# Queries, keys and values of three heads moved into the gate units, attention moved beside the r projection

## The chip, the cores and the metric

The kernel runs on one core of a Trainium2 chip. The metric is device microseconds of one execution. Each core has a matrix engine (PE, with its weight loads PEld), a vector engine (DVE), an activation engine (ACT), a general engine (POOL), and SyncE (SP), which here issues all DMAs, in program order.

## The reference

One encoder layer, 1024 tokens by 1024 channels, float32. Cut to what matters here:

```python
h = rmsnorm(x, norm_mix)
q, k, v, r, lr_f, lr_b, u, g_a, g_b = split(h @ w_in)     # 512 512 1024 1024 16 16 512 1024 1024
log_a_f = log_sigmoid(lr_f @ w_decay_up_fwd + b_decay_fwd) / 16      # and _b
# 4 heads of 128 keys and 256 values
o = gla_chunked(qh, kh, vh, af, include_diag=True) + flip(gla_chunked(flip(qh), flip(kh), flip(vh), flip(ab), False))
o = o * rsqrt(mean(o * o) + EPS) * gla_norm * silu(r)
y_a = o @ w_branch_gla
y_b = pooled(u) @ w_pool_group * pool_scale
x = x + (sigmoid(g_a) * y_a + sigmoid(g_b) * y_b) @ w_out
x = x + swiglu(rmsnorm(x, norm_ffn), w_ffn_in, w_ffn_out)
return rmsnorm(x, norm_final)
```

`gla_chunked` needs, per head and direction, the running sum of `log_a` within each chunk of 64, its exponentials on q and k, a masked score product, and a state carried from chunk to chunk.

## The kernel before

A float32 product is made of three matmuls on values split into a high and a low part (hi x hi, lo x hi, hi x lo): `products` and `mm3` (L268 to L275). A weight tile is loaded raw, cast to its high part on ACT (L197) and its difference taken on POOL or DVE (L198).

The work before the branch projection comes in this order on PE:

- Norms of the eight token tiles, and v of head 0 token tile by token tile (`values`, L384: 24 matmuls of 256 columns for a tile).
- The low-rank product `lrT` (L449), 32 matmuls.
- For each head h: q and k (`project_qk`, feature-major, 24 matmuls of 512 columns for each half of the tokens), then v of heads 1 to 3 by `values`. `attention(h)` is begun beside them as a side generator.
- r (`feature_major`, eight column tiles, two halves each), with the gated output (`gated`, L966: transposes of the head's output, one DVE operation) and the loads of the heads' outputs, which went to HBM (`o_out`).
- Ten gate units (u0, u1, four of g_A, four of g_B), each two column tiles wide. A unit computes a 2 x 2 block product (two column tiles, two halves of h's 1024 channels against two halves of the tokens) with seven half-size products instead of eight, each of 12 matmuls of 512 columns. Products 1 to 7 need sums and differences of weight blocks (fs, L882, on DVE) and of blocks of h (`right`). `Ahead` runs the weights' preparation some steps ahead (five). Pooling and the remaining sums run beside the units as generators.
- `project(0, BRANCH, ...)`: the branch projection by the same scheme, with blocks of `ob`, the gated output, as the left operand.

Four mechanisms set where other work stands. `pump(dt)` (L158) is called after every few matmuls and advances three lists: `pending` weight splits; `aside`, jobs on DVE, ACT and POOL with a pace (a new job every so many units of `dt`, only while no split is pending); and `side`, generators whose `yield` gives the wait in the same units until their next step. `finish_side` and `finish_beside` emit all that is left at once. `later` puts a DMA on a list and `flush` issues the list on SP. An engine runs its instructions in the order they were emitted; a DMA that must wait holds what stands behind it on SP.

`beside` (L572) runs a list of jobs: `branch_jobs` and `output_jobs` each make four generators, whose sums (wsum, L600, on POOL) of weight blocks go to HBM (`s_out`, `t_wo`) and are loaded by the branch and output projections; `feature_jobs` makes the sums of blocks of h (`hs`, `trh`, `trl`, L585 and L600, on DVE) that the units use as their right-hand side.

`attention(h)`: for each half and direction `decay` (z matmul, scan on DVE), `exponentials`, `apply_decay` (qe, ke), transposed keys (kt), a backward sweep over the chunks that saves the states (sb), then the forward sweep that makes the output (op, o), with its square sum, and `rms_scale` (ors, on POOL, L303).

Of the kernel before, what the change touches and what calls it, by code (L numbers as in the profile page):

```python
# [17 lines left out]
P = 128  # L18
D = 1024
SEQ = 1024  # L20
KT = D // P
# [30 lines left out]
def kernel(  # L52
# [354 lines left out]
    v = value_slots()  # L407
    norm_x(0)
# [34 lines left out]
    prepare()  # L443
    lrT = slot(F32R, (2, HALF), "lrT")
    for half in range(2):
        ps = bank(ps_mm)
        for k in range(KT):
            for i in range(2):
                nc.tensor.matmul(  # L449
                    ps[:, :], lw[k // 4][:, k % 4, :, :].rearrange("p a r -> p (a r)"), hT(k, half)[i],  # L450
                    start=k == 0 and i == 0, stop=k == KT - 1 and i == 1,
                )
            pump(2 / 3)
        nc.scalar.copy(lrT[:, half, :], ps[:, :])
        nc.vector.tensor_tensor(lrT[64:96, half, :], ps[64:96, :], as_f32(lrT[64:96, half, :]), op=ALU.subtract)


# [9 lines left out]

# [150 lines left out]
    v_heads, o_heads, unscaled = {}, {}, []  # L618
    HOLD, SCORES = 4.4, 6

    def project_qk():
        q = slot(s="q")
        k = slot(s="k")
        for dst, scale in ((q, DK**-0.5), (k, 1.0)):
            w = take()
            for half in range(2):
                ps = feature_major(w, hT, half)
                nc.scalar.activation(dst[:, half, :], ps[:, :], AF.Copy, scale=scale)
        return q, k

    def attention(h, q, k):


        qe = [slot(s="qe") for _ in range(2)]
        ke = [slot(s="ke") for _ in range(2)]
        fac = {}
        runs = ((1, 1), (0, 1), (0, 0), (1, 0))
        zs, las = {}, {}
        for half, d in runs:
            z = bank(ps_g, "z")  # L640
            nc.tensor.matmul(z[:, :], up[:, h, d, :], lrT[:, half, :], start=True, stop=True)
            bias = b_dec[d][:, h : h + 1]
            la = t2(s="la")
            nc.vector.tensor_scalar(la[:, :], z[:, :], bias, 0.0, op0=ALU.add, op1=ALU.min)
            nc.scalar.activation(z[:, :], z[:, :], AF.Abs, bias=bias)
            zs[half, d] = z
            las[half, d] = la
            yield 1.3
        for run in runs:
            nc.scalar.activation(zs[run][:, :], zs[run][:, :], AF.Exp, scale=-1.0)  # L650
        if unscaled:
            unscaled.pop()()
        yield 3.5
        flush()
        for run in runs:
            nc.scalar.activation(zs[run][:, :], zs[run][:, :], AF.Ln, bias=1.0)
        yield 6.5

        totals = {}

        def decay(half, d):
            la, z = las[half, d], zs[half, d]
            nc.vector.tensor_tensor(la[:, :], la[:, :], z[:, :], op=ALU.subtract)
            cs = z
            tot = vec(8, "tot")
            cs3 = cs.rearrange("p (n c) -> p n c", c=SUB)
            la3 = la.rearrange("p (n c) -> p n c", c=SUB)
            cy = carry.rearrange("p n c -> p (n c)")
            if d == 0:
                nc.vector.tensor_tensor_scan(cs[:, :], cy, la[:, :], 0.0, op0=ALU.mult, op1=ALU.add)  # L670
                nc.vector.tensor_copy(tot[:, :], cs3[:, :, SUB - 1])
            else:

                nc.vector.memset(cs[:, 0:1], 0.0)
                nc.vector.tensor_tensor_scan(  # L675
                    cs[:, 1:], la[:, : HALF - 1], cy[:, 1:], 0.0, op0=ALU.add, op1=ALU.mult
                )
                nc.vector.tensor_tensor(tot[:, :], cs3[:, :, SUB - 1], la3[:, :, SUB - 1], op=ALU.add)
            first = cs.rearrange("p (n a c) -> p n a c", a=2, c=SUB)[:, :, 0, :]
            tot2 = tot.rearrange("p (n a) -> p n a", a=2)  # L680
            nc.vector.tensor_tensor(first, first, tot2[:, :, 0:1].broadcast_to([P, 4, SUB]), op=ALU.subtract)
            totals[half, d] = tot

        def exponentials(half, d):
            cs, tot, e_q = zs[half, d], totals[half, d], qe[half]
            f = vec(12, "fac")
            sign = INV_NORMALIZER if d == 0 else -INV_NORMALIZER
            nc.scalar.activation(e_q[:, d, :], cs[:, :], AF.Exp, scale=sign)
            nc.scalar.activation(cs[:, :], cs[:, :], AF.Exp, scale=-sign)
            nc.scalar.activation(f[:, :8], tot[:, :], AF.Exp, scale=INV_NORMALIZER)  # L690
            fac[half, d] = f

        def apply_decay(half, d):
            f, e_q, e_k = fac[half, d], qe[half], ke[half]
            f2 = f[:, :8].rearrange("p (n a) -> p n a", a=2)
            nc.vector.tensor_tensor(e_k[:, d, :], zs[half, d][:, :], k[:, half, :], op=ALU.mult)
            nc.gpsimd.tensor_tensor(e_q[:, d, :], e_q[:, d, :], q[:, half, :], op=ALU.mult)
            nc.gpsimd.tensor_tensor(f[:, 8:], f2[:, :, 0], f2[:, :, 1], op=ALU.mult)

        def factor(n, d, which):  # L700
            f = fac[n // 4, d]
# [8 lines left out]

        def transposed_keys(half, d):
            kp = bank(ps_g, "kp")
            for i in range(4):
                nc.tensor.transpose(kp[:, i * P : (i + 1) * P], chunk_of(ke, 4 * half + i, d), ident[:, :])
            kt = slot(F32R, s="kt")
            split_to(kt[:, 0, :], kt[:, 1, :], kp[:, :])
            return kt
# [32 lines left out]
        decay(1, 1)  # L750
        yield HOLD
        exponentials(1, 1)
        decay(0, 1)
        yield 2
        apply_decay(1, 1)
        yield HOLD - 2
        exponentials(0, 1)
        decay(0, 0)
        yield 2
        apply_decay(0, 1)  # L760
        yield HOLD - 2
        exponentials(0, 0)
        kts = {(1, 1): transposed_keys(1, 1)}
        yield 1.5
        apply_decay(0, 0)
        decay(1, 0)
        yield HOLD
        while h not in v_heads:
            yield 0.5
        v = v_heads[h]  # L770

        def value(n):
            return tuple(part[:, n % 4, :] for part in v[n // 4])

        sb = [slot(shape=(4, DV), s="sb") for _ in range(2)]
        old = None
        for n in range(NT - 1, 0, -1):
            state, old = advance(old, n, 1, kts[n // 4, 1])
            m = n - 1
            nc.scalar.activation(  # L780
                sb[m // 4][:, m % 4, :], state, AF.Copy, scale=factor(m, 1, "before")
            )
            if n == 7:
                exponentials(1, 0)
            elif n == 5:
                apply_decay(1, 0)
            yield 1.2
            if n == 7:
                kts[0, 1] = transposed_keys(0, 1)
                yield 0.5  # L790
            if n == 2:
                kts[0, 0] = transposed_keys(0, 0)
                yield 0.5
# [5 lines left out]
        for n in range(NT):  # L799
# [18 lines left out]
            if n == 0:  # L818
                yield 0.38
                kts[1, 0] = transposed_keys(1, 0)  # L820
# [5 lines left out]
            yield 1.02  # L826
        rs = rms_scale(ms[:, :], NT, "ors")
        if h == HEADS - 1:
            o_heads[h] = o

        def normalize():
# [3 lines left out]
            if h < HEADS - 1:  # L835
                for half in range(2):
                    later(o_out[h][:, 4 * half : 4 * half + 4, :], o[half][:, :, :])

        unscaled.append(normalize)
        if h == HEADS - 1:  # L840
            unscaled.pop()()

    o_out = [dram.tile([P, NT, DV], F32, name=f"o_out{h}") for h in range(HEADS - 1)]

    def load_o(h):
        o_heads[h] = [slot(shape=(4, DV), s="ol") for _ in range(2)]
        for half in range(2):
            nc.sync.dma_start(o_heads[h][half][:, :, :], o_out[h][:, 4 * half : 4 * half + 4, :])

    for h in range(HEADS):  # L850
        qk = project_qk()
        begin(attention(h, *qk))
# [1017 lines left out]
```

## Time and profile before

| | |
|---|---|
| three runs | 1397.41, 1399.39, 1399.9 us |
| median | 1399.39 us |
| span of the profiled execution | 1400.4 us |
| matrix engine's matmuls | 6677 |
| DMA | 243.62 MB, mean 174 GB/s |

Its stages on PE: to 45 us norms and v of head 0; to 52 low rank; to 74 q, k of head 0; to about 335 heads, with attention; to 390 the rest of r; to 598 gate units; then branch, output projection and FFN. Durations of one matmul in groups are its latency; how fast they follow each other is seen in chains.

### The profile page before, as it was taken

What the parts mean: (1) busy time and instruction counts of PE and PEld (TensorE: products, weight loads), DVE (VectorE), ACT (ScalarE), POOL (GpSimd) and SP (SyncE); (2) the same over time, 40 slices, a digit from 0 to 9 for tenths busy, and PEclk for the clock granted to TensorE, in tenths of its full rate; (3) what the DMA queues carried; (4) which work ended last, traced back from release to release, by engine and by line L of the source; (5) the groups of instructions that cost most, each with busy time, mean ns of one, the idle gap of its engine ahead of it and who ended that gap; (6) DMA issues with size and microseconds to landing.
All of it is one profiled execution on the core that took longest, in us unless ns stands there. A gap on an engine that the chain in (4) does not pass through costs nothing.

```text
span 1400.4 us, 18571 instructions
## 1 busy us (share of the span) xinstructions
PE 1371.4 (98%) x6677; PEld 1157.4 (83%) x6677; DVE 854.4 (61%) x1073; ACT 624.6 (45%) x1119; POOL 750.4 (54%) x558
## 2 busy tenths in 40 slices
PE   7999999999999999999999999999999999999997
PEld 6889898988888878788887888888888888888876
DVE  6256857677745975587874865556565556343363
ACT  6364655554334444455346633333333334453253
POOL 3251616132288456468665176666666667454354
PEclk9999999999999999999999999999999999999999
DMA  6212413222368667996524455554444447975461
GB/s 193 76 45 61 136 59 107 89 79 71 125 207 286 199 220 235 346 407 233 194 76 173 173 180 174 173 173 156 145 142 148 140 153 255 388 255 218 165 234 67
DMA packets 167612, 243.62 MB, mean 174 GB/s; under 512 B 10936, under 2 KB 98016, under 8 KB 167520
## 3 DMA queue, kind: packets, MB, share of 16 engines
q1 hardware_dynamic: 167520, 242.45, 51.2%
q8 instruction: 52, 0.85, 0.2%
q14 instruction: 40, 0.33, 0.1%
HBM read 164.55 MB, written 77.86 MB: 173 GB/s over the span
## 4 chain that ended last, share of the span: by engine, by line
PE 81%; DVE 7%; ACT 4%; issue 3%; POOL 2%; DMA 2%; SPq 0%; POOLq 0%; DVEq 0%; ACTq 0%
PE ps L271 73%; PE op L813 2%; POOL wl L198 1%; PE kv L271 1%; PE sc L741 1%; PE op L271 1%; DVE z L670 1%; PE yb L271 1%; PE tr L318 1%; PE ps L449 1%; PE tp L972 1%; DMA gor<-g_out 0%; DMA wor<-t_out 0%; DVE z L675 0%; DMA u_out<-uph 0%
## 5 line engine op out<-in xcount | busy, mean ns | idle before, releaser
L198 POOL TENSOR_TENSOR wl<-fs,wh 128x512 fp32r<-128x512 f32 x120 | 165.9, 1386 | 163.4 <-ACT wh L197 138.1
L271 PE MATMUL ps<-gl,wh 128*128 128x512 f32 x616 | 239.8, 389 | 0.9 <-DVE gl L1462 0.9
L271 PE MATMUL ps<-gh,wh 128*128 128x512 f32 x616 | 240.4, 390 | 0.0
L271 PE MATMUL ps<-gh,wl 128*128 128x512 f32 x616 | 239.7, 389 | 0.0
L198 POOL TENSOR_TENSOR wl<-fraw,wh 128x512 fp32r<-128x512 f32 x90 | 129.1, 1435 | 63.9 <-ACT wh L197 63.9
L271 PE MATMUL ps<-hh,wh 128*128 128x512 f32 x376 | 150.4, 400 | 0.0
L198 POOL TENSOR_TENSOR ol<-gor,oh 128x1024 fp32r<-128x1024 f32 (+1 forms) x42 | 100.3, 2394 | 93.1 <-ACT oh L197 86.0
L271 PE MATMUL ps<-hh,wl 128*128 128x512 f32 x376 | 146.9, 391 | 0.0
L271 PE MATMUL ps<-hl,wh 128*128 128x512 f32 x376 | 146.8, 390 | 0.0
L198 POOL TENSOR_TENSOR wl<-raw,wh 128x512 fp32r<-128x512 f32 x47 | 64.4, 1382 | 152.8 <-ACT wh L197 141.4
L271 PEld LDWEIGHTS ps<-gl,wh 128*128 128x128 f32 x616 | 115.7, 188 | 25.0 <-DVE gl L1462 1.3
L271 PEld LDWEIGHTS ps<-gh,wl 128*128 128x128 f32 x616 | 115.7, 188 | 24.2
L271 PEld LDWEIGHTS ps<-gh,wh 128*128 128x128 f32 x616 | 115.7, 188 | 23.6
L271 PE MATMUL ps<-oh,oh 128*128 128x512 f32 x308 | 119.9, 389 | 1.3 <-DVE x L1792 1.3
L271 PE MATMUL ps<-ol,oh 128*128 128x512 f32 x308 | 119.9, 389 | 0.2 <-DVE ol L198 0.2
L271 PE MATMUL ps<-oh,ol 128*128 128x512 f32 x308 | 119.8, 389 | 0.0
L198 POOL TENSOR_TENSOR wl<-wraw,wh 128x512 fp32r<-128x512 f32 x56 | 90.9, 1653 | 45.4 <-ACT wh L197 36.1
L198 DVE TENSOR_TENSOR ol<-wor,oh 128x1024 fp32r<-128x1024 f32 (+1 forms) x42 | 62.0, 1496 | 53.9 <-ACT oh L197 46.6
L197 ACT CAST wh<-fs 128x512 fp32r<-128x512 f32 x120 | 73.8, 615 | 28.4 <-DVE fs L882 28.3
L271 PEld LDWEIGHTS ps<-hh,wl 128*128 128x128 f32 x376 | 70.8, 188 | 15.3
L271 PEld LDWEIGHTS ps<-hl,wh 128*128 128x128 f32 x376 | 71.1, 189 | 13.5
L271 PEld LDWEIGHTS ps<-hh,wh 128*128 128x128 f32 x376 | 71.1, 189 | 13.2
(251 smaller groups left out, 3197.4 us busy)
## 6 DMA issues: line engine op xcount, KB each, us to landing
fraw<-in_w_ffn_in_dram SPq DMA_DIRECT2D x44, 512.0 KB, 6.1
gor<-g_out SPq DMA_DIRECT2D x35, 512.0 KB, 6.3
raw<-in_w_in_dram SPq DMA_DIRECT2D x48, 256.0 KB, 3.1
g_out<-s SPq DMA_DIRECT2D x44, 256.0 KB, 2.3
fraw<-in_w_in_dram SPq DMA_DIRECT2D x20, 512.0 KB, 6.5
wor<-t_out SPq DMA_DIRECT2D x20, 512.0 KB
g_out<-g SPq DMA_DIRECT2D x33, 256.0 KB, 2.6
x<-in_x_dram SPq DMA_DIRECT2D x16, 512.0 KB, 4.9
```

The lines of the kernel that those rows point to most:

```text
L197: nc.scalar.copy(hi, src)
L198: eng.tensor_tensor(lo, src, as_f32(hi), op=ALU.subtract)
L271: nc.tensor.matmul(ps, a[i], b[j], start=first and n == 0, stop=last and n == 2, skip_group_check=onto)
L318: nc.tensor.transpose(ps[:, c], xt[:, k * P : (k + 1) * P], ident[:, :])
L449: nc.tensor.matmul(ps[:, :], lw[k // 4][:, k % 4, :, :].rearrange("p a r -> p (a r)"), hT(k, half)[i], start=k == 0 and i == 0, stop=k == ...
L670: nc.vector.tensor_tensor_scan(cs[:, :], cy, la[:, :], 0.0, op0=ALU.mult, op1=ALU.add)
L741: nc.tensor.matmul(sc[d][:, i * CH : (i + 1) * CH], chunk_of(ke, n, d), chunk_of(qe, n, d), start=True, stop=True,)
L813: nc.tensor.matmul(op[:, :DV], a, b, start=False, stop=j == len(terms) - 1)
L972: nc.tensor.transpose(tp[:, i * P : (i + 1) * P], o_heads[j // 2][half][:, i, (j % 2) * P : (j % 2 + 1) * P], ident[:, :],)
```

## The change

q, k and v of heads 1 to 3 become units among the gate units: 16 units, in the order u0, u1, q1 to q3 (each q and k of a head), v1 to v3, four of g_A, four of g_B. A q or v unit stores its results like a gate unit does; a v unit is transposed back to token-major by `turn` (16 transposes, one split) and put to HBM (`v_out`), q and k go to `qk_out`. The decays of all heads are made by a side generator, `decays`, beside the units and put to HBM (`dec_out`, 32 DMAs). r comes after the units, and the attention of all four heads beside it: `load_head`, `load_values` and `apply_decay` of the next head are called in the forward sweep of the one before. Half 1 of h is put to HBM (`h_out`) at the start and loaded back for r. The feature sums run beside low rank and q, k of head 0; `branch_jobs` and `output_jobs` run beside r, at pace 3. The outputs of heads 2 and 3 stay on chip for the branch projection. `Ahead` runs three steps ahead instead of five, and a unit's raw weights are loaded after product index 3, behind the flush, instead of index 0.

```diff
-    order = []
-    for h in range(HEADS):
-        cols_of = [(Q0 + h * DK, DK), (K0 + h * DK, DK), (V0 + h * DV, DV)]
-        order += [(w_in, KT, *c) for c in (cols_of if h else cols_of[2:] + cols_of[:2])]
-    order += [(w_in, KT, R0 + j * P, P) for j in range(KT)]
-    order = iter(order)
+    order = iter(
+        [(w_in, KT, c0, width) for c0, width in ((V0, DV), (Q0, DK), (K0, DK))]
+        + [(w_in, KT, R0 + j * P, P) for j in range(KT)]
+    )
...
-    prepare()
-    lrT = slot(F32R, (2, HALF), "lrT")
...
+    for half in range(2):
+        for n, part in enumerate(v[half]):
+            later(v_out[0][n][:, 4 * half : 4 * half + 4, :], as_f32(part[:, :, :]))
+    for kp in range(2):
+        for n, part in enumerate(hT.pair(kp, 1)):
+            later(h_out[kp][n], as_f32(part[:, :, :]))
+    flush()
...
+    def decays():
+
+        for h in range(HEADS):
+            for half in (1, 0):
...
+                for d in (1, 0):
+                    for n, t in enumerate((cums[d], las[d])):
+                        nc.sync.dma_start(dec_out[h][half][n][:, d, :], t[:, :])
+                yield 10
...
+            if h + 1 < HEADS:
+                if n == 2:
+                    load_head(h + 1)
+                if n == 4:
+                    load_values(h + 1, 1)
+                if 4 <= n < NT:
+                    apply_decay(h + 1, *RUNS[n - 4])
+                if n == NT - 1:
+                    load_values(h + 1, 0)
+                    kt_of[h + 1] = transposed_keys(h + 1, 1, 1)
+            yield STEP
         rs = rms_scale(ms[:, :], NT, "ors")
...
-    for h in range(HEADS):
-        qk = project_qk()
-        begin(attention(h, *qk))
-        if h == 0:
-            prepare_beside(map(branch_jobs, range(4)), 6)
-        if h > 0:
-            v = value_slots()
-            w = take()
-            for t in range(NT):
-                values(w, v, t)
-        v_heads[h] = v
...
+    kinds = [("u", i) for i in range(2)] + [("q", h) for h in range(1, HEADS)] + [("v", h) for h in range(1, HEADS)]
+    kinds += [(kind, i) for kind in "ab" for i in range(KT // 2)]
...
+    SUMS = 2.1
+    prepare_beside([feature_jobs(0), feature_jobs(1)], SUMS)
+    prepare()
+    lrT = slot(F32R, (2, HALF), "lrT")
...
+    project_qk(first_unit)
     finish_beside()
+    for _ in range(AHEAD - 3):
+        gates_ahead.step()
+    flush()
...
+        def turn(self, half):
+
+            hi, lo = slot(F32R, (4, DV), "vh"), slot(F32R, (4, DV), "vl")
+            for pair in range(2):
+                ps = bank(ps_g, "vt")
+                for t in range(2):
+                    for i in range(2):
+                        nc.tensor.transpose(
+                            ps[:, (2 * t + i) * P : (2 * t + i + 1) * P],
+                            self.row(i)[:, half, (2 * pair + t) * P : (2 * pair + t + 1) * P], ident[:, :],
+                        )
+                src = ps.rearrange("p (t c) -> p t c", t=2)
+                split_to(hi[:, 2 * pair : 2 * pair + 2, :], lo[:, 2 * pair : 2 * pair + 2, :], src[:, :, :])
+            for n, part in enumerate((hi, lo)):
+                later(v_out[self.at][n][:, 4 * half : 4 * half + 4, :], as_f32(part[:, :, :]))
...
-    for _ in range(AHEAD - 2):
-        gates_ahead.step()
-    flush()
+    begin(decays(), 4)
...
-            for _ in range(2 * (at == 0 and not last)):
-                gunits[n + 1].load()
...
-            if at == 4:
+            if at == 3:
                 flush()
...
+            for _ in range(2 * (at == 3 and not last)):
+                gunits[n + 1].load()
...
             if last and at == 1:
-                load_block(0, 0)
-                line_load()
-                line_load()
-                load_block(1, 0)
...
+                fetch()
+                load_head(0)
+            elif last and at == 4:
+                load_values(0, 1)
+                load_values(0, 0)
+                prepare()
...
+    for kp in range(2):
+        hT.tiles[kp, 1] = tuple(slot(F32R, s="h" + s) for s in "hl")
+        for n, t in enumerate(hT.tiles[kp, 1]):
+            nc.sync.dma_start(as_f32(t[:, :, :]), h_out[kp][n])
...
+    for h in range(HEADS):
+        begin(attention(h))
+    prepare_beside(chain(map(branch_jobs, range(4)), map(output_jobs, range(4))), 3)
+    for j in range(KT):
+        w = take()
+        r = slot(s="r")
+        for half in range(2):
+            ps = feature_major(w, hT, half)
+            flush()
+            nc.scalar.activation(r[:, half, :], ps[:, :], AF.Silu)
+            silu_r.append((j, half, r[:, half, :]))
+            for _ in range(2):
+                put_by()
+            if j == KT - 1:
+                if half == 0:
+                    finish_beside()
+                    load_block(0, 0)
+                    line_load()
+                    line_load()
+                else:
+                    load_block(0, 1)
+    finish_beside()
     project(0, BRANCH, collect_branch, before_branch)
```

More of the change, by code (lines that the diff above doesn't have):

```diff
@@ L442 @@
             low_rank_weights()
-    prepare()
-    lrT = slot(F32R, (2, HALF), "lrT")
[L445 to L455, printed above, removed]
     deferred = []
@@ L626, in project_qk @@
+    heads, v_heads, o_heads = {}, {}, {}
+    SCORES = 6
+    def project_qk(amid):
+        qk = [slot(s=s) for s in "qk"]
+        for dst, scale in zip(qk, (DK**-0.5, 1.0)):
+            w = take(dst is qk[0])
             for half in range(2):
+                amid(dst is qk[1], half)
                 ps = feature_major(w, hT, half)
                 nc.scalar.activation(dst[:, half, :], ps[:, :], AF.Copy, scale=scale)
[L629 to L653, printed above, removed]
-        flush()
[L655 to L698, printed above, removed]
@@ new lines, in project_qk, with load_head @@
+        for n, t in enumerate(qk):
+            later(qk_out[0][n], t[:, :, :])
+    def load_head(h):
+        q, k = (slot(s=s) for s in "qk")
+        qe, ke = {}, {}
+        for t, src in ((k, qk_out[h][1]), (q, qk_out[h][0])):
+            nc.sync.dma_start(t[:, :, :], src)
+        for half in (1, 0):
+            for n, (e, s) in enumerate(((qe, "qe"), (ke, "ke"))):
+                e[half] = slot(s=s)
+                nc.sync.dma_start(e[half][:, :, :], dec_out[h][half][n])
+        heads[h] = q, k, qe, ke
@@ L700, in factor, with attention @@
+    kt_of = {}
+    def attention(h):
+        q, k, qe, ke = heads[h]
         def factor(n, d, which):
-            f = fac[n // 4, d]
+            f = facs[:, h, n // 4, d, :]
             i = n % 4
@@ L709, in chunk_of @@
             return e[n // 4][:, d, (n % 4) * CH : (n % 4 + 1) * CH]
[L711 to L717, printed above, removed]
         def advance(old, n, d, kt):
@@ L748, in scores @@
             return hi, lo
[L750 to L770, printed above, removed]
-        def value(n):
-            return tuple(part[:, n % 4, :] for part in v[n // 4])
+        def value(n):
+            return tuple(part[:, n % 4, :] for part in v_heads[h][n // 4])
+        if h == 0:
+            for run in RUNS:
+                apply_decay(0, *run)
+                yield 1.5
+            kt_of[0] = transposed_keys(0, 1, 1)
+            yield 2
+        kts = {(1, 1): kt_of.pop(h)}
         sb = [slot(shape=(4, DV), s="sb") for _ in range(2)]
@@ L834, in normalize, with transposed_keys @@
                 nc.vector.tensor_scalar(t, t, rs[:, n : n + 1], None, op0=ALU.mult)
[L835 to L848, printed above, removed]
-    for h in range(HEADS):
-        qk = project_qk()
-        begin(attention(h, *qk))
-        if h == 0:
-            prepare_beside(map(branch_jobs, range(4)), 6)
-        if h > 0:
-            v = value_slots()
-            w = take()
-            for t in range(NT):
-                values(w, v, t)
-        v_heads[h] = v
+            o_heads[h] = o
+        soon(2, normalize)
+    STEP = 1.2
+    def transposed_keys(h, half, d):
+        ke = heads[h][3]
+        kp = bank(ps_g, "kp")
+        for i in range(4):
+            nc.tensor.transpose(kp[:, i * P : (i + 1) * P], ke[half][:, d, i * CH : (i + 1) * CH], ident[:, :])
+        kt = slot(F32R, s="kt")
+        split_to(kt[:, 0, :], kt[:, 1, :], kp[:, :])
+        return kt
     class Unit:
@@ L962 @@
     gates_ahead = Ahead(gunits, chain(*(steps_of(n, n == len(gate_units) - 1) for n in range(len(gate_units)))))
-    raw_r, oT = [], {}
-    def gated(j, half, src):
-        sr = t2(s="sr")
-        nc.scalar.activation(sr[:, :], src, AF.Silu)
-        tp = bank(ps_g, "tp")
-        for i in range(4):
-            nc.tensor.transpose(
-                tp[:, i * P : (i + 1) * P],
-                o_heads[j // 2][half][:, i, (j % 2) * P : (j % 2 + 1) * P], ident[:, :],
-            )
-        if j // 2 not in oT:
-            oT[j // 2] = [slot(s="o") for _ in range(2)], []
-        tiles, there = oT[j // 2]
-        nc.vector.scalar_tensor_tensor(
-            tiles[half][:, j % 2, :], tp[:, :], g_gla[:, j : j + 1], sr[:, :], op0=ALU.mult, op1=ALU.mult
-        )
-        there.append((j, half))
-        if len(there) == 4:
-            c = j // 2 % 2
-            for half, t in enumerate(tiles):
-                later(ob_out[j // 4, half][:, 2 * c : 2 * c + 2, :], t[:, :, :])
@@ L988, in put_by @@
-    def put_by():
-        if raw_r:
-            gated(*raw_r.pop(0))
-    BY = 3
-    sums_begun = False
-    for j in range(KT):
-        if 2 <= j <= 4:
-            load_o(j - 2)
-        w = take()
-        if j == 6:
+    SUMS = 2.1
[3 more added lines that the diff above has]
+    for half in range(2):
+        ps = bank(ps_mm)
+        for k in range(KT):
+            for i in range(2):
+                nc.tensor.matmul(
+                    ps[:, :], lw[k // 4][:, k % 4, :, :].rearrange("p a r -> p (a r)"), hT(k, half)[i],
+                    start=k == 0 and i == 0, stop=k == KT - 1 and i == 1,
+                )
+            pump(2 / 3)
+        nc.scalar.copy(lrT[:, half, :], ps[:, :])
+        nc.vector.tensor_tensor(lrT[64:96, half, :], ps[64:96, :], as_f32(lrT[64:96, half, :]), op=ALU.subtract)
@@ L1000, with first_unit @@
+    def first_unit(k, half):
+        if k and half == 0:
             for _ in range(2):
                 gunits[0].load()
[L1002 removed]
+        elif k:
             gates_ahead.step()
[L1004 to L1022 removed]
+    project_qk(first_unit)
@@ L1250, in run @@
             if part:
-                nc.scalar.copy(self.row(part[0])[:, part[1], :], ps)
+                nc.scalar.activation(self.row(part[0])[:, part[1], :], ps, AF.Copy, scale=self.scale(part[0]))
                 return
@@ L1377, in load_gates @@
                 nc.sync.dma_start(tiles[c][:, :, :], src[:, 1 - j, k : k + 2, :])
-    u2, v2 = ([slot(s="sum") for _ in range(2)] for _ in range(2))
     def merge(i, j, m, ps, s):
```

197 lines of the change are left out of this document (135 added, 62 removed).

## The prediction

> **What bounds the kernel now.** I read the page's first part, then the chain of waits, then the windows by stage, then groups by shape.
>
> ```profile
> span 1400.4 us, 18571 instructions
> PE 1371.4 (98%) x6677; PEld 1157.4 (83%) x6677; DVE 854.4 (61%) x1073; ACT 624.6 (45%) x1119; POOL 750.4 (54%) x558
> ```
>
> PE is the bound. The span is 1.0 us above the median of the runs (1399.39); I work against the span and take 1.0 off at the end. "Busy" hides pauses, so what a matmul costs is read from the chain of waits, where unbroken stretches stand with their count (start, length, what):
>
> ```profile
> 45.08 7.28 PE ps L449 x32
> 52.36 22.44 PE ps L271 x99
> ...
> 165.80 1.08 PE ps L271 x9
> ...
> 334.23 0.88 PE tp L972 x8
> 335.11 5.46 PE ps L271 x24
> ...
> 390.44 78.92 PE ps L271 x348
> ...
> 597.79 73.19 PE ps L271 x323
> ```
>
> A 512-column matmul costs 78.92 / 348 = 0.2268 us, a 256-column one 1.08 / 9 = 0.12, a transpose 0.88 / 8 = 0.11. The longer durations in the groups are latency. The branch projection begins at 597.79; everything the change touches lies before it.
>
> ```profile
> core 0: us, PE busy (x) PEld busy (x) DVE busy (x) ACT busy (x) POOL busy (x), PEclk, DMA share, GB/s
> 74.00:335.00 261.00, 257.17 (x1626) 232.82 (x1625) 179.03 (x343) 147.48 (x327) 99.91 (x84) 0.99 0.27 85
> 390.40:597.80 207.40, 204.18 (x890) 167.73 (x889) 131.59 (x148) 92.62 (x167) 134.61 (x103) 0.99 0.78 255
> 231.00:235.00 4.00, 3.60 (x12) 3.17 (x13) 3.83 (x7) 1.02 (x2) 3.92 (x4) 0.57 0.18 70
> 568.70:573.00 4.30, 4.25 (x12) 3.34 (x13) 0.88 (x2) 0.29 (x1) 3.08 (x4) 0.60 1.05 401
> ```
>
> In 74 to 335 (q, k, v of the heads with attention beside) the groups by shape, first and last of 16, are
>
> ```profile
> L271 PE MATMUL ps<-hh,wh 128*128 128x512 f32 x152 | 62.2, 409 | 0.0
> ...
> L972 PE MATMUL tp<-ident,ol 128*128 128x128 f32 x8 | 1.0, 272 | 0.0
> ```
>
> By width they are about 470 of 512 columns, 950 of 256 and 200 of 128: 470 x 0.2268 + 950 x 0.12 + 200 x 0.11 = 243 us. So 18 us of the 261 are lost. In 390.4 to 597.8 the 890 matmuls are worth 202 us, about 5.5 lost. **So PE loses some 23.5 us before the branch; this is all that better cover could return.** The named waits are few:
>
> ```profile
> PE kv L271 <- DVE kt L198: 3.4, 3, 2.1
> ...
> PE yb L271 <- DMA ph<-p_out: 1.0, 1, 1.0
> ...
> PE yb L271 <- DMA pl<-p_out: 0.8, 1, 0.8
> ```
>
> **The work removed.** Per head, 192 matmuls of 256 columns (v) and 96 of 512 (q, k) become two units of 7 x 12 = 168 of 512. Over three heads -576 x 0.12 = -69.1 and +216 x 0.2268 = +49.0. The v units come out feature-major and are turned back: 48 transposes, +5.3. Sum **-14.8 us**, from counts. The group that shrinks (256 before, 64 after, in each of three products):
>
> ```profile
> L271 PE MATMUL ps<-wh,hh 128*128 128x256 f32 x256 | 79.9, 312 | 0.0
> ```
>
> **The start.** Before, SP's list shows weight loads from 24.94 to 56.5 us, eight of them, those of q long landed; and ACT's list has q's cast while the low-rank product was on PE:
>
> ```profile
> 24.94 31.57 SPq L205 DMA_DIRECT2D raw<-in_w_in_dram  x8
> ```
>
> ```profile
> 49.26 0.62 ACT L197 CAST wh<-raw 128x512 fp32r<-128x512 f32 x1
> ```
>
> After, SP meets four puts of v and four of h (512 KB each) ahead of q's weight loads. The last two v puts wait for v's last split, at about 46. Six puts, 3 MB, at the 401 GB/s of the full stretch above are 7.8 us; the loads are issued near 48.2, share the transfers, and land at about 55.5 to 56, with the cast 57. q would have begun at 52.36, so PE waits about 5 us (bounds 1 and 7). Behind that cast on ACT stands the low-rank copy.
>
> The right-hand sums for unit 0 are made beside this stretch now, on DVE, where before they ran beside r:
>
> ```profile
> L600 DVE TENSOR_TENSOR hs<-hs,hs 128x1024 f32<-128x1024 f32 x8 | 11.8, 1481 | 0.2
> ...
> L600 DVE TENSOR_TENSOR hs<-hh,hl 128x1024 f32<-128x1024 f32 x8 | 10.7, 1351 | 0.0
> ...
> L585 DVE TENSOR_TENSOR trl<-hs,trh 128x1024 fp32r<-128x1024 f32 x8 | 10.6, 1342 | 8.6 <-DMA ob_out<-o 5.6 <-ACT trh L594 3.1
> ```
>
> 24 operations, 33.1 us, begun near 58 behind the late cast: the last pair is ready at about 90. Without loss PE would start unit 0 at 74 and read that pair near 78, with 5 us of the first wait at 83: 7 more. Start together **+12** (4 to 14).
>
> **The units before r.** Six units of q, k, v: weights' differences are on POOL and DVE as in the gate units, which lost nothing in the 78.92 us row; but each turn waits for an ACT copy and a split, like kt. By that row a wait is 3.4 / 3 = 1.1: three v units **+3.4** (0 to 7). The a and b units lose 5.5 now; the steps ahead fall from 5 to 3, the next weights are asked for three products later and behind the flush, and the decays' 32 puts precede. A few waits of the size of ph and pl: **+3** (-2 to +8).
>
> **Start of r.** Half 1 of h is loaded back, on SP behind the last yb puts:
>
> ```profile
> yb_out<-ga SPq DMA_DIRECT2D x8, 512.0 KB, 7.5
> ```
>
> The last put has its data some 3 us after the last product (sigmoid, gating, both behind the sum); issue 1.5 and a landing of about 6, less than the 7.5 since fewer are under way, make 10.4; r's half 0, which has its input on chip, covers 5.9 (24 matmuls and the first of the scan). **+4.5** (0 to 8).
>
> **Attention beside r.** Its DVE need per head: now 179.03 / 4 = 44.8, less the decays, less v's split, plus the gated output:
>
> ```profile
> L670 DVE TENSOR_TENSOR_SCAN z<-carry,la 128x512 f32<-128x512 bf16 x8 | 14.4, 1802 | 0.3
> L675 DVE TENSOR_TENSOR_SCAN z<-la,carry 128x511 f32<-128x511 f32 x8 | 13.8, 1731 | 0.3
> ...
> L644 DVE TENSOR_SCALAR la<-z,cols 128x512 f32<-128x512 f32 x16 | 11.7, 746 | 22.4 <-PE z L641 22.4
> ...
> L979 DVE SCALAR_TENSOR_TENSOR o<-tp,cols,sr 128x512 f32<-128x512 f32 x16 | 11.3, 742 | 5.7 <-ACT sr L969 5.2 <-ACT wh L197 0.5
> L198 DVE TENSOR_TENSOR vl<-ps,vh 128x256 fp32r<-128x256 f32 x32 | 13.3, 421 | 21.5 <-ACT vh L197 21.2
> ```
>
> Scans 7.1, two la passes (the second taken as long as the quoted one) some 6.0, v 2.5, gated +3.0: 32.2 per head. PE's work beside it, counted: r 384 x 0.2268 = 87.1, 376 of 256 columns 45.1, 256 of 128 28.2, together 160.4, and 149 until the last head's last output: 37.3 per head. DVE is 86% needed, against 179.03 / 261 = 69% before. No decays in the chain, but more density: I take **-2** of the 18 lost (-10 to +10).
>
> **The end of r.** This decides. Eight sum generators (four of the branch, four of the out weights) run beside r at pace 3; four operations each on POOL, and each one's loads on SP queue behind the puts of the one before. When the last half of r begins, three are not done: 12 operations. POOL takes them in program order, behind head 3's ors power, which needs head 3's last output; after that output PE has 42 wide matmuls and 16 transposes left, 42 x 0.2268 + 16 x 0.11 = 11.3 us. SP holds the first ob and weight loads of the branch behind the last put.
>
> ```profile
> L600 POOL TENSOR_TENSOR wsum<-wsum,wsum 128x512 f32<-128x512 f32 x16 | 22.7, 1420 | 0.5
> L600 POOL TENSOR_TENSOR wsum<-wsum 128x512 f32<-128x512 f32 x16 | 21.5, 1344 | 0.4
> ...
> L303 POOL TENSOR_TENSOR ors<-ors,half_neg 128x8 f32<-128x8 f32 x4 | 6.6, 1652 | 74.5 <-DVE ors L302 74.5
> ```
>
> ```profile
> DMA to landing us min/median/max: 2.4/3.5/7.7
> ```
>
> The second row is the landing of wsum's transfers. Chain: square, ors and power 3.0; two operations 2.8; the next loads, issue and landing, 4.4; two operations 2.8; loads 4.4; four operations 5.5; two ob and two weight loads 6.4; cast and difference 1.2: 30.5, less 11.3, is **+19** (12 to 25; 6.4 is the least sure, since
>
> ```profile
> ob<-ob_out SPq DMA_DIRECT2D x8, 512.0 KB, 10.8
> ```
>
> shows longer). Before, these loads were issued some 18 us ahead of 597.8, in the last unit, so PE passed without a stop. ob of heads 2 and 3 stay on chip, which spares 2 MB behind this, where nothing waits.
>
> **The clock.** In 231 to 235 PE, after its 2.1 us wait for kt, was granted 0.57 on average: half clock for about 3.4 us, which costs 1.7. The same followed the ph and pl waits (0.60). New long stops are the start, r's start and r's end; in the first the second wait swallows the slow time: 2 x 1.7 = **+3.4** (0 to 7).
>
> [...]
>
> **Sum.** -14.8 + 12 + 3.4 + 3 + 4.5 - 2 + 19 + 3.4 = +28.5: span 1428.9, time 1427.9; the larger terms can share cover (late PE gives DMA time), so I take about 3 off: **1425**. The likeliest case's own range is 1410 to 1441.
>
> **Rivals.**
> - *SP's order does not bind.* All three stops (start, r's start, r's end) are loads behind puts. If the puts' data is ready some 10 us before the loads are needed, all go: 1428 - 12 - 4.5 - 19 - 3.4 = 1389, **faster**. For it: pieces of 512 KB often land in 3 to 5 us. Against: at r's end the puts' data hangs on POOL behind ors, and ors on PE. It decides from chain under 11.3 us. Chance 0.15.
> - *Only the end is covered* (POOL's operations pass ahead of ors in time, or fewer remain): 1425 - 21 = 1404, from 1394 to 1410. Chance 0.17, half of it above +0.2%.
> - *DVE becomes the bound beside r.* At 86% need, with its waits for POOL's products and reloaded decays, each head takes 4 us more: +16, about 1441 to 1455. For it the 3.4 us kt waits at 69%; against, r's matmuls are interleaved as filler. Chance 0.13.
> - *The saving itself is not there* (half products bring waits of their own for their split and adds): the 78.92 us row speaks against, 348 in a row without a pause. It would be 1440, inside the upper part. Chance 0.03.
>
> **Numbers.** Forecast 0.52. Slower: 0.52 + 0.13 + 0.03 + 0.09 = 0.77; within 0.2% (2.8 us, about what a measurement can tell): 0.05; faster: 0.15 + 0.03 = 0.18. The range 1392 to 1446 leaves out the first rival's lower half and the third's upper half, under 2 in 10.
>
> **What would show it.** Matmul groups of 64 x 256 columns and PE's count 312 lower; PE waiting for ACT's wh cast after low rank, for DVE's low part (trl) in unit 0, for hh and hl loads at r's start; above all a gap of 12 to 25 us at the head of the branch, with POOL in wsum and ob loads issued after its last put. Wrong if that gap is under 5 us, if PE before it passes the start without 4 us, or if attention beside r loses more than 30 us.

## The result and the profile after

| | median of the runs | ratio to before, 95% interval |
|---|---|---|
| before | 1399.64 us (1397.41 to 1401.53, 4 runs) | |
| after | 1517.45 us (1513.69 to 1518.15, 4 runs) | 1.0845 (1.0824 to 1.0866) |

The change makes the kernel 118 us slower. The forecast was slower, but by 25 us. First the page of the changed kernel:

```profile
span 1516.4 us, 18227 instructions
PE 1399.6 (92%) x6365; PEld 1145.4 (76%) x6365; DVE 881.5 (58%) x1103; ACT 649.5 (43%) x1138; POOL 768.9 (51%) x576
```

PE has 312 matmuls fewer, as counted (6677 to 6365), and is at 92% of a longer span instead of 98%. No other engine is full: DVE fell from 61% to 58%. So nothing became the bound by amount; PE waits. The windows by stage say where. Their edges are the first matmul of unit 0 that reads the new sums (94.7), the last of the units (470.5), the end of r (674.4), the first branch product (689.4) and the first FFN product (871.7):

```profile
core 0: us, PE busy (x) PEld busy (x) DVE busy (x) ACT busy (x) POOL busy (x), PEclk, DMA share, GB/s
45.10:94.70 49.60, 35.42 (x146) 28.00 (x144) 34.09 (x28) 14.59 (x21) 9.91 (x6) 0.89 0.45 143
94.70:470.50 375.80, 342.43 (x1437) 267.30 (x1438) 213.94 (x288) 200.01 (x350) 178.62 (x148) 0.97 0.55 183
470.50:674.40 203.90, 185.52 (x1023) 158.90 (x1022) 127.75 (x245) 74.16 (x176) 79.10 (x60) 0.95 0.58 194
674.40:689.40 15.00, 0.28 (x3) 0.04 (x1) 2.58 (x3) 1.72 (x4) 5.05 (x4) 0.60 0.85 297
689.40:871.70 182.30, 167.96 (x704) 134.89 (x705) 123.48 (x124) 82.26 (x135) 112.12 (x71) 0.94 0.50 179
871.70:1516.40 644.70, 633.29 (x2805) 522.99 (x2803) 351.49 (x351) 247.60 (x391) 372.83 (x242) 1.00 0.54 186
```

The same windows of the kernel before, from the first branch product on, show that the FFN is the same and the branch is not:

```profile
597.80:756.30 158.50, 156.55 (x704) 129.08 (x704) 121.41 (x125) 80.65 (x131) 109.59 (x69) 1.00 0.58 213
756.30:1400.40 644.10, 633.32 (x2805) 523.15 (x2803) 351.24 (x351) 249.03 (x392) 373.74 (x242) 1.00 0.54 186
```

With the matmul costs of the prediction each stretch can be split into work and loss. Units: 1389 wide matmuls and 48 transposes are 320 us, so 56 of 376 are lost (the gate units of before lost 5.5). r with attention: 160 of work, 43.5 lost (18 in the heads before). End of r: 15 us with nothing on PE. Branch and out projection: the same 704 matmuls take 23.8 us more. The start: 146 wide matmuls are 33 of 49.6 us, 16.5 lost, where before nothing was. Against before that is 50 + 25.5 + 15 + 23.8 + 16.5 - 14.8 of saved work = 116, which is the difference of the spans, 1516.4 - 1400.4.

The waits of PE name what came last (total, times, longest):

```profile
PE ps L269 <- ACT wh L197: 43.6, 13, 14.8
PE ps L269 <- POOL wl L198: 20.2, 32, 1.3
PE ps L269 <- DVE dl L162: 11.2, 5, 3.4
PE kv L269 <- ACT kt L197: 9.7, 2, 9.4
```

None of the first three is a bound of these engines. A cast takes 0.6 us and ACT is at 43%. Of the 43.6 us, 14.8 are the end of r and 4.8 the first weights of q, where the cast itself waited for a load; 9.3 are the wait before the new sums. The 13.9 in the units are a queue: the cast is late because of what ACT or DVE had to do before it. What that looks like is shown by ACT's and DVE's timelines of the changed kernel, and then PE's (start, length, engine, line, operation, in brackets the idle time before it and what ended it):

```profile
157.98 0.61 ACT L197 CAST wh<-fraw 128x512 fp32r<-128x512 f32 x1
162.15 1.28 ACT L654 ACT_TABLE_LOAD   x1 [3.55 <-issue]
163.44 0.63 ACT L654 ACTIVATE la<-cum 128x512 f32<-128x512 f32 x1
...
165.72 0.63 ACT L654 ACTIVATE la<-cum 128x512 f32<-128x512 f32 x1 [0.88 <-DVE cum L649]
166.38 0.63 ACT L655 ACTIVATE cum<-cum 128x512 f32<-128x512 f32 x1
166.92 0.19 ACT L656 ACTIVATE facs<-tot 128x8 f32<-128x8 f32 x1
167.01 0.60 ACT L197 CAST wh<-fs 128x512 fp32r<-128x512 f32 x1
```

```profile
161.66 0.43 DVE L649 TENSOR_TENSOR cum<-cum,tot 128x256 f32<-128x256 f32 x1
...
163.20 0.68 DVE L858 TENSOR_TENSOR fs<-fraw 128x512 f32<-128x512 f32 x1
163.80 1.22 DVE L638 TENSOR_TENSOR_SCAN cum<-carry,la 128x512 f32<-128x512 bf16 x1
```

```profile
167.67 0.50 PE L269 MATMUL ps<-trh,wh 128*128 128x512 f32 x1 [2.91 <-ACT wh L197]
...
169.62 0.63 PE L269 MATMUL ps<-trh,wh 128*128 128x512 f32 x1
170.04 0.63 PE L269 MATMUL ps<-trl,wh 128*128 128x512 f32 x1
```

The sum fs is ready at 163.88. Its cast is emitted behind the exponentials of the decays, of which the second pair waits for a scan on DVE. So ACT casts at 167.01, 3.1 us after it could, and PE has stood for 2.9. The decays held ACT's line for longer than these 3.1 us. Its cast before that one ended at 158.59. From there ACT stood 3.55 us, while DVE finished the first scan (its last step ended at 162.09), then loaded a table for 1.28 and made the exponentials: 8.4 us without a cast. PE had two prepared products when that began, at 2.7 us each. After the wait PE goes at half clock (granted 0.50 from 169.0 to 172.2): 169.62 to 170.04 is 0.42 for one matmul instead of 0.227.

At the end of r the chain of waits (start, length, what) goes as the prediction laid it out:

```profile
657.54 1.64 POOL ors L301
659.18 1.25 POOL wsum L588
...
660.51 1.27 POOL wsum L588
...
662.65 5.53 DMA wsum<-in_w_out_dram
...
669.99 4.80 DMA wsum<-in_w_out_dram
...
681.70 7.04 DMA wraw<-in_w_branch_gla_dram
...
690.79 1.22 PE ps L269 x2
```

### The profile page after: what moved, and what is told of

Read it like the earlier page. It is cut to its first block, busy times and chain, and to the rows that moved or that the text cites. A ratio compares the mean times of both kernels' runs of the same rounds, so it can differ in the third digit from the quotient of the medians.

```text
span 1516.4 us, 18227 instructions
## 1 busy us (share of the span) xinstructions
PE 1399.6 (92%) x6365; PEld 1145.4 (76%) x6365; DVE 881.5 (58%) x1103; ACT 649.5 (43%) x1138; POOL 768.9 (51%) x576
## 4 chain that ended last, share of the span: by engine, by line
PE 49%; issue 5%; POOL 4%; DVE 4%; DMA 3%; ACT 1%; SPq 0%; POOLq 0%; DVEq 0%; ACTq 0%
PE ps L269 47%; POOL wsum L588 1%; POOL wl L198 1%; DMA wsum<-in_w_out_dram 1%; DVE res L1798 1%; DMA ke<-dec_out 1%; DMA wor<-t_out 1%; DVE dl L162 0%; DMA wraw<-in_w_branch_gla_dram 0%; PE tr L1512 0%; POOL qe L698 0%; PE kv L269 0%; DVE xn L305 0%; DMA wsum<-in_w_branch_gla_dram 0%; POOL n3rs L1564 0%
## 5 line engine op out<-in xcount | busy, mean ns | idle before, releaser
L198 POOL TENSOR_TENSOR wl<-fs,wh 128x512 fp32r<-128x512 f32 x144 | 201.1, 1400 | 225.3 <-ACT wh L197 197.1
L198 POOL TENSOR_TENSOR wl<-fraw,wh 128x512 fp32r<-128x512 f32 x108 | 153.1, 1417 | 120.5 <-ACT wh L197 97.9
L269 PE MATMUL ps<-hh,wl 128*128 128x512 f32 x352 | 141.6, 402 | 3.7 <-POOL wl L198 2.9
L269 PE MATMUL ps<-hl,wh 128*128 128x512 f32 x352 | 140.9, 400 | 0.0
L269 PE MATMUL ps<-trh,wh 128*128 128x512 f32 x256 | 103.4, 404 | 18.6 <-ACT wh L197 18.6
L269 PE MATMUL ps<-trh,wl 128*128 128x512 f32 x256 | 104.8, 409 | 14.3 <-POOL wl L198 14.2
L269 PE MATMUL ps<-trl,wh 128*128 128x512 f32 x256 | 101.8, 398 | 0.0
L197 ACT CAST wh<-fs 128x512 fp32r<-128x512 f32 x144 | 88.4, 614 | 28.5 <-DVE fs L858 26.0
L198 POOL TENSOR_TENSOR wl<-raw,wh 128x512 fp32r<-128x512 f32 x23 | 32.5, 1426 | 114.1 <-ACT wh L197 110.6
```

The source lines that it names most:

```text
L197: nc.scalar.copy(hi, src)
L198: eng.tensor_tensor(lo, src, as_f32(hi), op=ALU.subtract)
L269: nc.tensor.matmul(ps, a[i], b[j], start=first and n == 0, stop=last and n == 2, skip_group_check=onto)
```

## The experiments

Each is one program on the chip, compared by its stretches. Where one kernel ran four times, its times lie up to 5 us apart (1425.8 to 1430.8 in run 11, 1397 to 1401 before), so a few us between single times say nothing. Ahead of each measurement stands the text written before the run.

**1. The decays' arithmetic left out.** `decays` keeps its 32 puts and its pace; the z matmuls, scans and exponentials go, and a constant is put.

```diff
-                    nc.tensor.matmul(z[:, :], up[:, h, d, :], lrT[:, half, :], start=True, stop=True)
...
-                        nc.vector.tensor_tensor_scan(cs[:, :], cy, la[:, :], 0.0, op0=ALU.mult, op1=ALU.add)
...
+                t = t2(s="la")
+                nc.vector.memset(t[:, :], 1.0)
```

> Leaves out the arithmetic of the decays beside the units (z matmuls, scans, exponentials); constants take their place and the 32 puts stay. In the changed kernel the stretch from the first unit matmul (94.5 us) to r (472) is 378 us, for about 324 us of matmuls. Theory A (decays stand in line on ACT and DVE ahead of the weights' sums and casts): the stretch falls to 340 us or less. Theory B (only three steps of preparation ahead, whatever stands beside): it stays above 360. Whole time by A about 1475, by B about 1500 or more.

Measured 1481.69 us; the stretch of the units 342.9, 33 less, of which the 16 z matmuls are 3.6. That is 3 us short of what theory A asked for; theory B alone is refuted.

```profile
94.10:437.00 342.90, 328.36 (x1422) 262.91 (x1423) 155.11 (x209) 132.09 (x238) 166.74 (x132) 0.99 0.60 200
```

**2. Five steps ahead.** The lead of the weights' preparation as before, which needs the raw weights at product 0.

```diff
-    for _ in range(AHEAD - 3):
+    for _ in range(AHEAD - 1):
         gates_ahead.step()
...
+            for _ in range(2 * (at == 0 and not last)):
+                gunits[n + 1].load()
             if at == 3:
                 flush()
-            for _ in range(2 * (at == 3 and not last)):
-                gunits[n + 1].load()
```

> Five steps ahead again and the next unit's weights asked for at product 0, as in the kernel before; the decays stay. Theory B: the stretch of the units falls from 378 to 340 us or less and the waits for POOL's wl (17 us in 26) vanish. Theory A alone: it stays above 360. If both matter, 345 to 365.

Measured 1477.47; 341.2 us for the units with all the decays in them, between what was set for B (340) and for both (345). Theory A alone is refuted:

```profile
92.80:434.00 341.20, 328.73 (x1436) 269.25 (x1437) 219.70 (x288) 198.50 (x350) 177.29 (x148) 0.98 0.60 197
```

Waits for wl in the whole run fell from 20.2 us in 32 to 3.7 us in 7, and past the one before the new sums PE waits for no cast in the units. ACT's line is held there as before: its longest stretch without a cast in the units is 8.9 us, from 189.97 to 198.89.

**3. The loads alone at product 0.** The second half of that edit.

> Only the place of the next unit's loads goes back to product 0, ahead of the flush. Theory C (raw weights arrive late behind the flush): the stretch falls by 10 us or more. Theories A and B: by less than 4 us, since the sums of the weights waited for their data only 12 us in four places.

Measured 1521.32; the units took 383.5 us, 7.7 more than after; the whole time is 3.9 us more, inside the spread of repeated runs. The place of the loads is not the cause (theory C falls), and run 2 owes its gain to the lead.

**4. Neither decays nor the short lead.** Edits 1 and 2 together.

> Leaves out the arithmetic of the decays as before, now with five steps ahead; compare the stretch of the units with 341 us (five steps, decays there) and 343 (three steps, no decays). If the two causes are one (decays are late work that a longer lead absorbs), the stretch falls only a little, to 332 to 340. If each costs its own 33 us, it falls to 310 to 320.

Measured 1464.12, the units 327.0:

```profile
94.30:421.30 327.00, 322.78 (x1421) 266.18 (x1422) 160.75 (x209) 131.63 (x238) 170.19 (x132) 0.98 0.63 205
```

Each cure alone takes 33 to 35 us off, both take 49, not 68: 327 lies between the 332 to 340 of one cause and the 310 to 320 of two. So A and B, put as alternatives in the expectations, share 19 us, over half of what either cure gives. Two times explain the shared part: the decays hold ACT's line for up to 8.4 us in the changed kernel (8.9 in run 2). With a lead of three PE has two prepared products left to run when the next cast becomes due, 5.4 us; with a lead of five it has four, 10.9 us (an estimate from 12 x 0.2268 = 2.72 us for a product). The second covers the longest holds and the first does not; this was worked out for the longest hold of each run, not for every wait. The decays' arithmetic costs 14 us even under the longer lead (341 - 327), of which the 16 z matmuls are 3.6.

**5. q's weights asked for ahead of the puts.** `fetch()` in the loop over the token tiles.

```diff
         if t == 4:
             low_rank_weights()
+            fetch()
```

> The raw load of q's weights is asked for ahead of the puts of v and h. By the prediction's step the first wait (4.9 us at 52) vanishes; the wait for the sums before unit 0 (9.4 us) shrinks with it, since they begin earlier: unit 0 starts at 82 to 88 instead of 94.5. Rival (the sums' wait is set by DVE's own length): unit 0 starts at 92 or later, and the time moves by less than 4 us.

Measured 1505.84: the second product of unit 0 at 84.5 instead of 94.7. The first wait is gone; the one for the sums shrank from 9.3 to 7.4. Inside the expectation.

**6. The feature sums at pace 1.2** (on top of run 11 below).

> As five_mended, with the sums of h at pace 1.2 instead of 2.1. If the wait before unit 0 (7.6 us left) comes from emission order, jobs handed out too late behind the weights, unit 0's second product starts 4 us earlier or more. If DVE's own length sets it (24 operations of 1.2 to 2.4 us), it moves by less than 2 us.

Measured 1430.88: the product began at 91.4, 8.6 us later than with 2.1 (82.8). Neither reading foresaw that. DVE's sums take as long at both paces (50.3 to 86.4 here, 48.4 to 83.5 in run 11). What moved is the cast of the unit's first weights, which read no sum: at pace 1.2 it stands on ACT behind the last high part of a sum (trh, at 84.06) and comes at 85.49, at pace 2.1 it came at 67.56. PE waits 11.9 us for it.

**7. Pace 2 for the sums beside r** (on top of run 2).

```diff
-    prepare_beside(chain(map(branch_jobs, range(4)), map(output_jobs, range(4))), 3)
+    prepare_beside(chain(map(branch_jobs, range(4)), map(output_jobs, range(4))), 2)
```

> On top of the run with five steps ahead (1477.5 us): the eight sum generators beside r at pace 2 instead of 3, so that fewer of POOL's operations are left behind head 3's ors. The prediction's theory of the end of r: the 15 us gap before the first branch product falls below 5, time about 1464 to 1468. Rival (the gap is the time of the loads of ob and branch weights alone): it stays above 10.

Measured 1466.42, 11 us less; the hole before the branch went from 14.9 to 1.5 us, at no cost to r (201.9 to 200.4). The loads of ob and weights, the rival, are then hidden. The branch took 184.8 instead of 182.3, so part of the gain came back there.

**8. The out weights' sums beside the units** (on top of run 2; branch sums alone beside r).

```diff
+        if n == 8:
+            prepare_beside(map(output_jobs, range(4)), 2.8)
...
-    prepare_beside(chain(map(branch_jobs, range(4)), map(output_jobs, range(4))), 3)
+    prepare_beside(map(branch_jobs, range(4)), 3)
```

> On top of five steps ahead: only the branch sums run beside r, the sums of the out weights beside the units from the ninth on, as the kernel before had them beside the units. The theory of the end of r: gap below 5 and time 1460 to 1468. The units may lose up to 5 for it. Rival (loads alone): gap above 10.

Measured 1484.44. The hole closed too (1.5), but the units took 363.5 instead of 341.2, 22 us where 5 were allowed. PE then waits for ACT and DVE on results (ga 9.7 and 4.8 us, vt 6.8). In the kernel before that work stood beside the ten gate units, which lost 5.5 us in all; beside units that already carry decays and turns it does not fit.

**9. The first two branch pieces ahead** (on top of run 8).

```diff
                 else:
                     load_block(0, 1)
+                    line_load()
+                    line_load()
+                    line_make()
+                    line_make()
```

> As the run before it, and the first two pieces of the branch projection (their loads, casts and differences) are made during the last half of r, as the kernel before made them in its last unit. Theory: the 23.6 us that the branch and out projections take longer (182.3 instead of 158.7 us from the first branch product to the first FFN product) come from pieces made one ahead instead of two or three, DVE's dl waits 11.2 us: the stretch falls to 158 to 166, time 1440 to 1450. Rival (the longer stretch comes from ob of heads 2 and 3 and their sums being late, or from DVE): it stays above 175.

Measured 1463.35, 21 us less. Branch and out projection without it (first row, run 8) and with it (second, this run):

```profile
654.30:840.30 186.00, 169.47 (x705) 135.67 (x706) 124.70 (x125) 82.31 (x135) 114.83 (x71) 0.94 0.43 148
```

```profile
653.90:818.50 164.60, 160.27 (x705) 131.15 (x706) 124.55 (x125) 83.47 (x135) 116.90 (x71) 0.98 0.48 162
```

Same work on all engines, 21.4 us apart: the lead again, for the left operands this time. PE's waits for the left operands' low parts (dl L162) fell from 11.1 us to 0.7 in this stretch. The time itself, 1440 to 1450, was missed by what run 8 lost in the units.

**10. All orders mended, on run 9.** Edit 5, and r's second weights asked for ahead of h's reload:

```diff
+    fetch()
     for kp in range(2):
         hT.tiles[kp, 1] = tuple(slot(F32R, s="h" + s) for s in "hl")
```

> As the run before it, with q's weights asked for ahead of the puts at the start (worth 11.6 alone) and r's second weights asked for ahead of h's reload. Theory: r's start loses its 9.4 us wait for kt, whose cast stands on ACT behind the cast of weights that SP has queued behind yb and h; sum 1420 to 1430. If the 9.4 us wait is for h itself, it stays and the time is 1430 to 1440.

Measured 1447.41, above the expected sum for the same reason as run 9. Of the 9.3 us for kt in run 9, 3.7 are left, and r falls from 194.1 to 188.0. ACT's timeline of the changed kernel shows why r's start stood: ACT sat 14 us for the raw weights, which SP had queued behind yb and h, with the cast of kt emitted behind it.

```profile
470.89 0.60 ACT L1214 ACTIVATE ga<-ps 128x512 f32<-128x512 f32 x1 [1.36 <-PE ps L269]
485.60 0.62 ACT L197 CAST wh<-raw 128x512 fp32r<-128x512 f32 x1 [14.12 <-DMA raw<-in_w_in_dram]
```

**11. The five edits that helped** (2, 5, 7, 9 and the fetch of 10).

> All repairs that helped together: five steps ahead with loads at product 0, pace 2 for the sums beside r, the first two branch pieces made ahead, q's and r's weights asked for early. From the runs before it: 1466.4 (pace 2) less 20 (pieces), less 9 to 10 (start), less 6 (r's start) = 1430; 1424 to 1436 if these add, above 1440 if they share. By the accounting of the prediction the kernel before stays faster; it is beaten only below 1397.

Measured 1425.94 us (1425.82 to 1430.82, 4 runs), ratio to before 1.0198 (1.0172 to 1.0225). Inside the 1424 to 1436 expected if they add. The change with its leads and orders mended is still 2% slower than the kernel before:

```profile
82.80:423.00 340.20, 328.04 (x1436) 268.59 (x1437) 217.89 (x288) 198.31 (x350) 177.66 (x148) 0.98 0.61 198
423.00:615.60 192.60, 181.48 (x1023) 156.20 (x1022) 129.49 (x245) 73.81 (x177) 84.59 (x64) 0.98 0.76 265
617.10:780.90 163.80, 160.22 (x705) 130.98 (x706) 124.61 (x125) 83.48 (x135) 116.97 (x71) 0.98 0.47 163
```

Over the work 20 us remain in the units, 32 beside r, some 7 at the start and 1.5 at the end of r, against the 23.5 of before; the branch takes 5 more than before. That is more than the 14.8 us that the products save.

**12. The turn of v put off** (on top of run 11): `soon(2, ...)` in place of `late.append`.

> As five_mended, with the transposes of the v units put off by two steps of the pump, so that PE does not stand in front of ACT's copy and DVE's sum. PE waited 8.9 us for vt in four places: if that is all, the units take 6 to 9 us less; if the wait moves on to the next product's weights, less than 3.

Measured 1434.88, the units 346.0 instead of 340.2: worse, a miss. The waits for vt were 9.1 us in four places; in run 11 they are 5.1 in three, not the 8.9 in four of the expectation. What delayed ACT's copies for them was not followed.

## Why the prediction was right or wrong

The sign was right and the size was not: +25 forecast, +118 measured, far above the range. Three steps failed: the units, the attention beside r and the branch, which were put at 6.4, -2 and 0 and measured 50, 16 and 23.8. Step by step:

- **Work removed**, -14.8: right. 312 matmuls fewer, and the work of each stretch agrees with the counts.
- **The start**, +12: measured 16.5, with both waits where they were put, 4.8 us for q's weights and 9.3 for the sums. Mechanism right (run 5), size short: DVE's sums ran from 58.7 to 95.4, to an end 5 us later than counted, and the matmuls between the waits lost 2.4, above all at half clock. The last step was not trl, as forecast, but ACT's cast of the unit's weights, behind the last high part of a sum.
- **The units before r**, +6.4 beside the 5.5 already lost: this step failed. The prediction counted of the decays only "32 puts" and of the shorter lead "a few waits of the size of ph and pl". It let the weights' differences run "as in the gate units, which lost nothing in the 78.92 us row". That row was under a lead of five and without decays on ACT and DVE. The prediction took the decays off the attention's DVE need and charged their arithmetic nowhere. It measured 56 lost, 50 more than before; runs 1, 2 and 4 show the pair of decays in line and a lead of three. The 3.4 set down for the turns did not come: no wait for vt is in the changed kernel's list (5.3 us in run 2).
- **The start of r**, +4.5: measured 9.4, and not a wait for h. SP's queue behind yb was right; what stood in it was the next weights, and their cast held the cast of kt on ACT.
- **Attention beside r**, -2 of 18 lost: this step failed too. Measured 43.5 lost in the stretch, 34 without the start of r, so 16 more than before; more than 30 was the prediction's own sign of being wrong. DVE's need was sized well (127.75 us, 32 for a head), and at 63% it was not the bound, against that rival. By the start times of the matmuls in the trace, stops over 0.15 us cost 20.6 us in the stretch (4.6 in the heads before), of which the start's is 9.4 and the other named ones are 9 (o, kt, sf); half clock costs 7 (1.6 before), shorter pauses 14 (11.5 before). So it is stops and the clock behind them that grew. The fetch of run 10 took most of the start's part away; 32 us are still lost beside r in run 11, and the cause of the rest stays open.
- **The end of r**, +19: measured 15.0, by the chain as laid out; run 7 confirms it. POOL had exactly the 12 operations left, and PE the 42 wide matmuls and 16 transposes. From the last output on, the chain took 33 us instead of 30.5 and its cover 18 instead of 11.3 (waits for o and half clock), so the two errors partly cancel.
- **The clock**, +3.4: too small. Counting the wide matmuls that follow each other at half pace, 116 of them took 23 us more, against 18 and 3.5 us before; this lies inside the losses above. The number of stops was mis-sized rather than the price of one: the trace grants half clock in 12 spells after 45 us and before the end, against 2 before, and 19.5 us more over 10 more spells, 1.95 each, is near the 1.7 forecast for one. The 2.9 us wait that ended at 167.67 was followed by half pace until 172.18 (granted 0.50 from 169.0 on). The shortest single wait that half clock followed is 2.25 us in the changed kernel (ended at 622.97, granted 0.50 until 626.0); before it was the 2.10 us one for kt, ended at 231.40, and two of 0.97 and 0.82 us close together (ended at 567.45 and 568.75) had it behind them too.
- **The branch**, 0: this step failed by the sentence "everything the change touches lies before it". The change also takes out two calls of `line_make` in the last gate unit (L1305 of the kernel before, in a part of the diff that is not printed), two of four `line_load` and two of four block loads. 23.8 us; run 9, with two calls of each of the first two put back, gives back 21.

Of the rivals, the one by which SP's order does not bind is refuted (three stops measured), and so are the covered end and DVE as the bound beside r. That half products bring waits of their own is not borne out: without decays and with a lead of five the units lose 10 of 327 us (run 4).

## What to carry to other kernels

A lead (steps prepared ahead, pieces made before a phase begins) is a price like a duration. When a change shortens one or puts work in line on an engine that feeds it, cost the two together, by the longest time that the line holds the next cast, against the prepared products left times the length of one. An engine at 43% can still be late for its casts, and a group that waited for nothing under the old lead says nothing of the new one. Read a diff's removed calls as closely as its added ones: two lost `line_make` calls, with their loads, cost 21 us here.

## What was not expected of the hardware

Half clock came after single stops as short as 2.10 us (before) and 2.25 us (after), though not after one of 2.55 us (after, ended at 805.28, granted 1.00 until 810), and added up: 116 wide matmuls at 0.43 us instead of 0.227, 23 us in all, against 3.5 before. The granted clock over the run was 0.97 after, 0.988 in the mended kernel and 0.996 before.
